# Sums of squares, the scaling of v and the um copies moved from VectorE to ScalarE in the gated-delta heads of a decoder trunk

## The chip, the cores and the metric

The kernel runs on one core of one Trainium2 chip, as one program in one launch. The metric is the device time of one execution in microseconds (us), as a median over several runs; lower is better. The engines are named as the profile names them: PE is TensorE (PEld its weight loads), DVE is VectorE, ACT is ScalarE, POOL is GpSimd, SP is the engine that issues most DMAs.

## What is computed

The reference is a two-layer decoder trunk on 512 tokens of width 1024. Layer 0 is a gated DeltaNet with 8 heads of width 128, layer 1 is differential attention on a shared K/V; each is followed by a squared-ReLU MLP of width 4096, and norms are modulated by a conditioning vector. The change touches layer 0 alone, and there the following:

```python
def l2norm(x):
    xf = x.astype(jnp.float32)
    return (xf * lax.rsqrt(jnp.sum(xf * xf, axis=-1, keepdims=True) + EPS)).astype(x.dtype)
...
    kb = kc * bc[..., None]
    a_mat = jnp.where(strict, jnp.einsum('bhnik,bhnjk->bhnij', kb, kc) * decay, 0.0)
    rhs = jnp.concatenate([vc * bc[..., None], kb * jnp.exp(gcum)[..., None]], axis=-1)
    sol = lax.linalg.triangular_solve(eye + a_mat, rhs, left_side=True, lower=True, unit_diagonal=True)
...
    o = gated_delta_rule(l2norm(q), l2norm(k), v, g, beta).astype(h.dtype)
    o = rmsnorm(o, out_g) * jax.nn.silu(z)
```

Each head therefore needs three sums of squares per token: of q and of k for the l2 norm, and of its output o for the RMS norm. It also needs the inverse of a unit lower-triangular matrix per chunk of tokens.

## The kernel before

Activations lie transposed, 128 features by 512 tokens a tile, in fp32. A projection is split in a high and a low part (fp32r): for each pair of 128-row weight blocks ACT rounds the raw weights to `wh` (L293), DVE or POOL forms the rest `wl` (L284), and PE does three matmuls of 128x512 (L300, L301, L302 in `three`). Raw weights come by SP's DMAs (L291) into three rotating buffers; a buffer is free again when its `wl` has been formed. Beside this runs a queue of dot products that make the modulation vectors (L193 on DVE, its weights by L189 on SP).

The work is not issued in the order of the source. The program is traced first; then a list scheduler with its own cost table puts the instructions of each engine into an order, and every engine runs its own order strictly. A changed instruction can thus shift the order of all engines.

For each of the 8 heads `proj_head(h)` does 72 projection matmuls for q, k and v into three PSUM banks `pj` (tag j has three), and `conv_silu` takes each bank through a four-tap causal convolution: one scaled copy on ACT (L481), three multiply-adds on DVE (L483), a Silu on ACT (L485). A bank is free for the next head only after its three L483. Then `gdn(h)` works in chunks of 128 tokens (the four 128-column units that `uu(t, n)` picks):

- A decay matrix `ex` from `gm` (POOL L528, ACT L531), a matmul (L532), Exp on ACT (L534) and a mask on POOL (L535).
- `natural` transposes k, v and q on PE into bank `pa` (L513; tag a has two banks). `sumsq` (L516) squares a 128x512 tile on ACT (L518) and sums each row per chunk on DVE (L520). It is called for k (`sqk`), q (`sqq`) and later o (`sqo`). Small column operations make `rk` (POOL L543), `sj` (L545, L546) and `nk` (L642); v is scaled by `nk` into `vn` (L648).
- Products of k with k and q (PE L554, L555), masked and scaled into `bq` (DVE L558). The 16x16 diagonal blocks `dc` (L570, L574) go to DRAM and back in another layout (SP L576, L578), are inverted by 15 steps of L584 and L586 on DVE, go through DRAM again (L589, L591), and are spread into the tile `t` (DVE L593).
- `t` is transposed on PE into `z` (L598, L600), and the inverse is doubled from blocks of 16 to 128: with PE products into `pu` (L605, L622), a copy of `pu` to `um` (L607, and L624 for blocks of 32 and 64), products with `z` (L610, L613, L628, L633) and subtractions on DVE (L614, L615, L635, L638). The copy L624 is two pieces of 32x128 and one of 64x256 a head.
- A recurrence over four chunks with the state `st`: five PE products a chunk (L670, L678, L679, L683, L684) with DVE (L676, L681, L688, L690, L660) and ACT (L674, L686) between them. Then the RMS norm of o (`sqo`, L696 to L702) and the output scale (L705 or L707).

While a head's chain runs, PE fills in with projection matmuls of later heads or of the gate (`gate`, L713). `close_block` then multiplies with `a_w_out`, for which `ogh` is made from all heads' outputs (L745).

Of the kernel before, what the change touches and what calls it, by code (L numbers as in the profile page):

```python
# [12 lines left out]
AF = mybir.ActivationFunctionType  # L13
ALU = mybir.AluOpType
AX = mybir.AxisListType
PSUM = bass.MemoryType.PSUM

P = 128
# [3 lines left out]
NT = S // P  # L22
# [63 lines left out]
def trunk_kernel(ctx: ExitStack, tc: tile.TileContext, a, outT):  # L86
    nc = tc.nc
    V, G, A, T = nc.vector, nc.gpsimd, nc.scalar, nc.tensor
# [3 lines left out]
    def nm(s):  # L92
        count[0] += 1
        return f"{s}_{count[0]}"
# [33 lines left out]
    def big(pool, tag, bufs, dt=F32):  # L128
        return pool.tile([P, S], dt, tag=tag, name=nm(tag), bufs=bufs)

    def col(n, name="c"):
        return tp.tile([P, n], F32, tag=f"{name}{n}", name=nm(name))

    def bank(tag):
        return pools["p"].tile([P, S], F32, tag=tag, name=nm("p" + tag), bufs=pools["n"][tag])

    def bc(ap, n):
        return ap.unsqueeze(2).to_broadcast([ap.shape[0], ap.shape[1], n])

    def v3(ap, n=P):  # L140
        return ap.rearrange("p (u f) -> p u f", f=n)
# [231 lines left out]
    for k in range(KT):  # L373
        n = NE[k]
        sq = acc[n]
        if k >= 3:
            sq = m_pool.tile([P, S], F32, tag=f"sq{n}", name=nm("sq"), bufs=2)
# [123 lines left out]
    def uu(t, n):  # L501
        return t[:, n * P:(n + 1) * P]

    def m4(ap):
        return ap.unsqueeze(1).to_broadcast([P, 4, P])
# [3 lines left out]
    def gdn(h):  # L509
        def natural(src, tag="a"):  # L510
            ps = bank(tag)
            for c in range(NT):
                T.transpose(uu(ps, c), uu(src, c), ident)  # L513
            return ps

        def sumsq(src, tag):  # L516
            sq = big(g_pool, {"sqq": "sqk"}.get(tag, tag), 1)
            A.activation(sq, src, AF.Square)  # L518
            ss = col(4, tag)
            V.tensor_reduce(out=ss, in_=v3(sq), axis=AX.X, op=ALU.add)  # L520
            return ss


# [14 lines left out]
        kn = big(g_pool, "kn", 3)  # L538
        A.activation(kn, pk, AF.Copy)
        ssk = sumsq(kn, "sqk")  # L540
        V.tensor_scalar(out=ssk, in0=ssk, scalar1=EPS, scalar2=None, op0=ALU.add)
        rk = col(4, "rk")
# [7 lines left out]
        for n in range(2):  # L550
# [5 lines left out]
            for c in (2 * n, 2 * n + 1):  # L556
                o = (c % 2) * 256
                V.scalar_tensor_tensor(out=v3(bq[n][:, o:o + 256]), in0=v3(ps[:, o:o + 256]), scalar=sj[:, c:c + 1],  # L558
                                       in1=uu(ex, c).unsqueeze(1).to_broadcast([P, 2, P]), op0=ALU.mult, op1=ALU.mult)

        def B(n):
            return bq[n // 2][:, (n % 2) * 256:(n % 2) * 256 + P]
# [6 lines left out]
        for n in range(2):  # L569
            V.tensor_tensor(out=v3(db[:, n * 256:(n + 1) * 256]),  # L570
                            in0=bq[n].rearrange("p (u t f) -> p u t f", u=2, t=2)[:, :, 0, :],
                            in1=m_sub.unsqueeze(1).to_broadcast([P, 2, P]), op=ALU.mult)
# [9 lines left out]
        for s in range(SUB - 1):  # L582
            shp = [32, SUB - 1 - s, s + 1]
            V.tensor_tensor(out=pr[:, s + 1:, :s + 1], in0=mt[:, s, s + 1:].unsqueeze(2).to_broadcast(shp),  # L584
                            in1=xv[:, s, :s + 1].unsqueeze(1).to_broadcast(shp), op=ALU.mult)
            V.tensor_tensor(out=xv[:, s + 1:, :s + 1], in0=xv[:, s + 1:, :s + 1], in1=pr[:, s + 1:, :s + 1],  # L586
                            op=ALU.subtract)
# [6 lines left out]
                        in0=tc_.unsqueeze(2).to_broadcast([P, 4, P // SUB, SUB]),  # L594
                        in1=m4(m_sub).rearrange("p u (b c) -> p u b c", c=SUB), op=ALU.mult)
# [7 lines left out]
        pu = bank("i")  # L603
        for n in range(4):
            T.matmul(uu(pu, n), lhsT=B(n), rhs=uu(t_, n), start=True, stop=True)  # L605
        um = big(g_pool, "um", 1)
# [9 lines left out]
        for b in (32, 64):  # L616
            parts = [(slice(lo, lo + b), slice(lo + b, lo + 2 * b)) for lo in ((0, 64) if b == 32 else (0,))]
            pu = bank("i")
            um = big(g_pool, "um", 1)
            for p0, p1 in parts:  # L620
                for n in range(4):
                    T.matmul(pu[p1, n * b:(n + 1) * b], lhsT=B(n)[p0, p1], rhs=uu(t_, n)[p0, p0], start=True, stop=True)  # L622
            for p0, p1 in parts:
                V.tensor_copy(um[p1, 0:4 * b], pu[p1, 0:4 * b])  # L624
            pz = bank("i")
            for p0, p1 in parts:
                for n in range(4):
                    T.matmul(pz[p0, n * b:(n + 1) * b], lhsT=um[p1, n * b:(n + 1) * b], rhs=uu(z, n)[p1, p1],  # L628
                             start=True, stop=True)
            if b == 32:  # L630
                p0, p1 = parts[0]
                for n in range(4):
                    T.matmul(pz[p1, n * b:(n + 1) * b], lhsT=uu(z, n)[p1, p1], rhs=um[p1, n * b:(n + 1) * b],  # L633
                             start=True, stop=True)
                V.tensor_tensor(out=v3(t_)[p1, :, p0], in0=v3(t_)[p1, :, p0],  # L635
                                in1=v3(pz[p1, 0:4 * b], b), op=ALU.subtract)
            for p0, p1 in parts:
                V.tensor_tensor(out=v3(z)[p0, :, p1], in0=v3(z)[p0, :, p1], in1=v3(pz[p0, 0:4 * b], b),  # L638
                                op=ALU.subtract)

        nk = col(4, "nk")
# [3 lines left out]
        G.tensor_tensor(out=v3(kn), in0=v3(kn), in1=bc(kd, P), op=ALU.mult)  # L645
        pv = natural(vT[h])
        vn = big(g_pool, "vn", 4)
        V.tensor_tensor(out=v3(vn), in0=v3(pv), in1=bc(nk, P), op=ALU.mult)  # L648

        ssq = sumsq(natural(qT[h]), "sqq")  # L650
        V.tensor_scalar(out=ssq, in0=ssq, scalar1=float(P), scalar2=EPS * P, op0=ALU.mult, op1=ALU.add)
        rq = col(4, "rq")
# [40 lines left out]
        yield  # L693

        so = sumsq(o, "sqo")
        V.tensor_tensor(out=so, in0=so, in1=rq, op=ALU.mult)  # L696
        V.tensor_tensor(out=so, in0=so, in1=rq, op=ALU.mult)
# [31 lines left out]
    for h in range(H):  # L729
        proj_head(h)  # L730
        heads.append(gdn(h))
        next(heads[h])
        next(heads[h])
        if h:
            next(heads[h - 1], None)
# [136 lines left out]
    scale = 128 ** -0.5  # L872
# [138 lines left out]
```

## Time and profile before

| what | value |
|---|---|
| median of 3 runs | 1384.9 us (1381.57 to 1387.92) |
| profiled execution, its own time | 1381.92 us |
| its span, first to last instruction | 1380.1 us |
| mean granted TensorE clock | 0.986 |
| busy: PE, PEld, DVE, ACT, POOL | 95%, 80%, 62%, 38%, 34% of the span |

The profile is of one execution. Its page gives busy time by engine, the same in 40 slices of 34.5 us, and the costliest groups of instructions. Further views of the trace answer by group of instructions (line, engine, operation, tiles, count, total busy time in us, mean of one in ns, then idle time before them and what ended it), by wait (who waited for whom: total us, times, longest), by stretch of time, and as a timeline. Times within the span are counted from its start. A busy PE is not a PE at its peak: matmuls are pipelined and their ends are modelled.

The stage of the change lies between about 84 us, when the first head's chain starts, and about 392 us, when the last head's output is scaled.

### The profile page before, as it was taken

The numbers are of one execution on the slowest core, as the hardware profiler recorded it, in microseconds if no ns is written. First come the engines' busy times: TensorE is split into PE (matmuls) and PEld (weight loads), VectorE is DVE, ScalarE is ACT, GpSimd is POOL, SyncE is SP. The second block draws the span as 40 slices with busy tenths as digits, with TensorE's granted clock in tenths as the row PEclk, the third lists the DMA queues.
The fourth block names the chain that finished last, engine by engine and source line by source line (L and its number), as shares of the span: only waits on it lengthen the run. The fifth ranks groups of instructions, "written<-read, shape, count | busy, mean of one in ns | idle before, by whom it ended". The sixth has DMA issues, their size and how long they took to land. (4 is left out here: it accounts for less than half of the span.)

```text
span 1380.1 us, 19204 instructions
## 1 busy us (share of the span) xinstructions
PE 1309.7 (95%) x7240; PEld 1101.4 (80%) x7240; DVE 850.9 (62%) x1688; ACT 529.1 (38%) x951; POOL 471.4 (34%) x281
## 2 busy tenths in 40 slices
PE   4887998999999999999999999999999999999997
PEld 3665787777789888888888987888798888888886
DVE  6989899899846987778861687777552110031113
ACT  3394344443424533225332354444344322143221
POOL 3324132222004544444444012232135444444441
PEclk9997999999999999999999999999999999999998
DMA  9632223225542776776753233222113233233221
GB/s 314 212 90 57 81 78 81 74 72 147 175 151 65 266 239 225 242 236 219 241 165 100 81 100 104 65 66 66 61 62 123 92 96 103 92 100 99 92 76 62
DMA packets 113212, 174.97 MB, mean 127 GB/s; under 512 B 16384, under 2 KB 56992, under 8 KB 113120
## 3 DMA queue, kind: packets, MB, share of 16 engines
q1 hardware_dynamic: 112416, 172.92, 39.5%
q8 instruction: 57, 0.93, 0.3%
q10 hardware_dynamic: 704, 0.83, 0.2%
q14 instruction: 35, 0.29, 0.1%
HBM read 170.04 MB, written 2.62 MB: 125 GB/s over the span
## 5 line engine op out<-in xcount | busy, mean ns | idle before, releaser
L284 POOL TENSOR_TENSOR wl<-raw,wh 128x1024 fp32r<-128x1024 f32 (+1 forms) x137 | 329.3, 2404 | 392.9 <-ACT wh L293 392.9
L293 ACT ACTIVATE wh<-raw 128x1024 fp32r<-128x1024 f32 (+2 forms) x217 | 216.0, 996 | 502.0 <-PE pj L301 250.1
L300 PE MATMUL pj<-h,wh 128*128 128x512 f32 (+1 forms) x816 | 290.9, 360 | 16.0 <-ACT h L278 5.5
L301 PE MATMUL pj<-h,wh 128*128 128x512 f32 (+1 forms) x816 | 292.6, 359 | 0.0
L302 PE MATMUL pj<-h,wl 128*128 128x512 f32 (+1 forms) x816 | 290.4, 358 | 1.1 <-DVE wl L284 1.1
L193 DVE SCALAR_TENSOR_TENSOR mw<-mw,one,cs 128x1024 f32<-128x1024 f32 x96 | 210.1, 2202 | 47.5 <-ACT one L213 47.2
L300 PEld LDWEIGHTS pj<-h,wh 128*128 128x128 f32 x816 | 155.9, 192 | 37.2 <-ACT h L278 7.5
L302 PEld LDWEIGHTS pj<-h,wl 128*128 128x128 f32 x816 | 156.6, 192 | 19.4 <-DVE wl L284 2.4
L301 PEld LDWEIGHTS pj<-h,wh 128*128 128x128 f32 x816 | 156.9, 192 | 17.9 <-DVE h L279 0.3
L301 PE MATMUL pj<-u,wh 128*128 128x512 f32 (+1 forms) x448 | 160.9, 359 | 0.0
L302 PE MATMUL pj<-u,wl 128*128 128x512 f32 (+1 forms) x448 | 160.9, 359 | 0.0
L300 PE MATMUL pj<-u,wh 128*128 128x512 f32 (+1 forms) x448 | 160.8, 359 | 0.0
L346 DVE SCALAR_TENSOR_TENSOR x<-pj,mod,x 128x256 f32<-128x256 f32 (+1 forms) x53 | 30.2, 584 | 152.2 <-PE pj L302 152.2
L284 DVE TENSOR_TENSOR wl<-raw,wh 128x1024 fp32r<-128x1024 f32 (+2 forms) x80 | 84.5, 1058 | 18.7 <-ACT wh L293 18.6
L300 PEld LDWEIGHTS pj<-u,wh 128*128 128x128 f32 x448 | 84.6, 189 | 12.7 <-issue 0.2
L301 PEld LDWEIGHTS pj<-u,wh 128*128 128x128 f32 x448 | 84.6, 189 | 12.5
L302 PEld LDWEIGHTS pj<-u,wl 128*128 128x128 f32 x448 | 84.6, 189 | 12.5
L767 DVE SCALAR_TENSOR_TENSOR pj<-pj,r 128x512 f32<-128x512 f32 x32 | 21.6, 690 | 52.2 <-ACT r L766 52.0
L301 PE MATMUL pn<-h,wh 128*128 128x512 f32 x128 | 49.8, 389 | 0.0
L300 PE MATMUL pn<-h,wh 128*128 128x512 f32 x128 | 49.8, 389 | 0.0
L300 PE MATMUL pm<-h,wh 128*128 128x512 f32 x128 | 49.8, 389 | 0.0
L302 PE MATMUL pm<-h,wl 128*128 128x512 f32 x128 | 49.8, 389 | 0.0
(298 smaller groups left out, 2371.7 us busy)
## 6 DMA issues: line engine op xcount, KB each, us to landing
raw<-in_mlp_w_dram SPq DMA_DIRECT2D x128, 512.0 KB, 3.7
mw<-in_mod_wT_dram SPq DMA_DIRECT2D x96, 512.0 KB, 4.7
raw<-in_a_w_in_dram SPq DMA_DIRECT2D x96, 128.0 KB, 2.6
mw<-in_kv_mod_wT_dram SPq DMA_DIRECT2D x16, 512.0 KB, 5.1
raw<-in_kv_w_dram SPq DMA_DIRECT2D x16, 512.0 KB, 3.3
x<-in_xT_dram SPq DMA_DIRECT2D x16, 256.0 KB, 6.0
raw<-in_a_w_in_dram SPq DMA_DIRECT2D x16, 256.0 KB, 2.9
raw<-in_a_w_out_dram SPq DMA_DIRECT2D x8, 512.0 KB, 4.3
```

What stands on the lines that cost most here:

```text
L193: V.scalar_tensor_tensor(out=w, in0=w, scalar=one, in1=cs, op0=ALU.mult, op1=ALU.mult, accum_out=raw_mod[:, c:c + 1])
L284: (V if n else G).tensor_tensor(out=out, in0=x, in1=hi.bitcast(F32), op=ALU.subtract)
L293: A.activation(wh, raw, AF.Copy)
L300: T.matmul(ps, lhsT=wh, rhs=xh, start=first, stop=False, skip_group_check=skip)
L301: T.matmul(ps, lhsT=wh, rhs=xl, start=False, stop=False, skip_group_check=skip)
L302: T.matmul(ps, lhsT=wl, rhs=xh, start=False, stop=last, skip_group_check=skip)
L346: V.scalar_tensor_tensor(out=x[d][:, sl], in0=ps[j][:, sl], scalar=mod[:, gt + d:gt + d + 1], in1=x[d][:, sl], op0=ALU.mult, op1=ALU.add)
L767: V.scalar_tensor_tensor(out=ps[j], in0=ps[j], scalar=0.0, in1=r, op0=ALU.max, op1=ALU.mult)
```

## The change

Four things move from DVE to ACT, all in `gdn`; nothing else is edited.

- `sumsq` no longer squares a whole tile on ACT and sums on DVE. ACT squares each of the four 128x128 chunks with an accumulated output, which is the sum. One ACT and one DVE instruction become four ACT instructions with an accumulator each.
- The copies of `pu` to `um` (L624) become ACT copies of the same shapes.
- The scaling of v into `vn`, one DVE multiply of 128x512, becomes four ACT copies of 128x128, each with a per-partition scale (L649 in the changed file; after it all line numbers are one higher).

```diff
         def sumsq(src, tag):
             sq = big(g_pool, {"sqq": "sqk"}.get(tag, tag), 1)
-            A.activation(sq, src, AF.Square)
             ss = col(4, tag)
-            V.tensor_reduce(out=ss, in_=v3(sq), axis=AX.X, op=ALU.add)
+            for c in range(NT):
+                A.activation(uu(sq, c), uu(src, c), AF.Square, accum_out=ss[:, c:c + 1])
             return ss
...
             for p0, p1 in parts:
-                V.tensor_copy(um[p1, 0:4 * b], pu[p1, 0:4 * b])
+                A.activation(um[p1, 0:4 * b], pu[p1, 0:4 * b], AF.Copy)
...
         vn = big(g_pool, "vn", 4)
-        V.tensor_tensor(out=v3(vn), in0=v3(pv), in1=bc(nk, P), op=ALU.mult)
+        for c in range(NT):
+            A.activation(uu(vn, c), uu(pv, c), AF.Copy, scale=nk[:, c:c + 1])
```

The heads still come in the same order, but the scheduler puts out another order within each engine. Three places follow. In them a name is that of a tile with its running number, so numbers differ between the two programs for the same tile.

First PE, at the first transpose of `t` (L598, head 0), before: `pj` are projection banks, `h` the activations, `cv` the convolved tiles, `wh` and `wl` the weight parts.

```order
L300 MATMUL pj_1475<-h_172,wh_1506 128x512
L513 MATMUL pa_1392<-mask,cv_1220 128x128 x4
L301 MATMUL pj_1475<-h_173,wh_1506 128x512
L513 MATMUL pa_1399<-mask,cv_1214 128x128 x4
L532 MATMUL pa_1608<-gm_1609,m_gtr 128x512
L532 MATMUL pa_1608<-gm_1612,m_gtr 128x512
L598 MATMUL pi_687<-mask,t_685 128x128 x4
L605 MATMUL pi_694<-t_685,bq_623 128x128 x2
```

The same place on PE in the changed program:

```order
L301 MATMUL pj_1498<-h_181,wh_1588 128x512
L302 MATMUL pj_1498<-h_180,wl_1590 128x512
L300 MATMUL pj_1498<-h_182,wh_1588 128x512
L301 MATMUL pj_1498<-h_183,wh_1588 128x512
L302 MATMUL pj_1498<-h_182,wl_1590 128x512
L598 MATMUL pi_689<-mask,t_687 128x128 x4
L605 MATMUL pi_696<-t_687,bq_625 128x128 x2
```

Before, PE comes to L598 in the middle of head 3's second block of weights; now it has done two of head 3's three banks with all four blocks. Counted over the whole order, 264 projection matmuls (L300 to L302) stand ahead of it before, and 306 now. No earlier or later head changes its turn.

Second DVE, at the first low part `wl` of head 3's weights, before (`pr`, `xv` and `mt` belong to the inversion of the 16x16 blocks):

```order
L541 TENSOR_SCALAR sqk_1248<-sqk_1248 128x4
L586 TENSOR_TENSOR xv_648<-xv_648,pr_649 32x8x8
L586 TENSOR_TENSOR xv_895<-xv_895,pr_896 32x15
L284 TENSOR_TENSOR wl_1482<-raw_1476,wh_1480 128x768
L584 TENSOR_TENSOR pr_649<-mt_646,xv_648 32x7x9
```

The same tile on DVE in the changed program:

```order
L483 SCALAR_TENSOR_TENSOR cv_1236<-pj_1105,cols,cv_1236 128x511
L546 TENSOR_TENSOR sj_876<-sj_876,beta 128x4
L284 TENSOR_TENSOR wl_1507<-raw_1501,wh_1505 128x768
L584 TENSOR_TENSOR pr_651<-mt_648,xv_650 32x15
L558 SCALAR_TENSOR_TENSOR bq_879<-pa_881,sj_876,ex_857 128x256
```

The cast has moved ahead of the whole inversion of head 0 and of head 1's `bq`. Counted from L475, the last instruction that all heads share, the first L593 is the 111th DVE instruction before and the 109th now; one `wl` stands between the two before, four now.

Third the copies `um` of head 0. Before they stood on DVE, behind the subtraction that follows the block-16 step:

```order
L615 TENSOR_TENSOR z_692<-z_692,pi_706 128x512
L624 COPY um_714<-pi_713 32x128 x2
L584 TENSOR_TENSOR pr_896<-mt_893,xv_895 32x2x14
L584 TENSOR_TENSOR pr_1282<-mt_1279,xv_1281 32x14x2
L193 SCALAR_TENSOR_TENSOR mw_1188,raw_mod<-mw_1188,one_1567,cs 128x1024
```

In the changed program they stand on ACT:

```order
L534 ACT_TABLE_LOAD
L534 ACTIVATE ex_1643<-pa_1633 128x512
L624 ACTIVATE um_716<-pi_715 32x128 x2
L293 ACTIVATE wh_1979<-raw_1975 128x768
L485 ACT_TABLE_LOAD
L485 ACTIVATE cv_1621<-cv_1621 128x512
L624 ACTIVATE um_744<-pi_743 64x256
```

The first two pieces stand behind an Exp with its table load, the third behind a weight cast and a Silu with its table load. Both programs hold 24 table loads in all.

## Prediction

> **What bounds the kernel now.** I read the page first, for its slices of the span.
>
> ```profile
> span 1380.1 us, 19204 instructions
> PE   4887998999999999999999999999999999999997
> DVE  6989899899846987778861687777552110031113
> ACT  3394344443424533225332354444344322143221
> PEclk9997999999999999999999999999999999999998
> ```
>
> PE is at nine tenths nearly everywhere, but its first slices are not, and these are the slices in which DVE is full (slice 3 to 11, some 70 to 390 us) and in which the granted clock drops once, to 7. Next I asked for stretches of time: the columns are length, then PE, PEld, DVE, ACT and POOL busy in us with their instructions, then granted clock, DMA share and GB/s.
>
> ```profile
> 90.00:130.00 40.00, 29.67 (x126) 22.66 (x124) 34.97 (x112) 24.33 (x45) 17.16 (x16) 0.79 0.16 39
> 130.00:400.00 270.00, 254.94 (x1734) 206.71 (x1735) 231.36 (x652) 111.91 (x203) 59.90 (x45) 0.98 0.39 111
> 400.00:1380.00 980.00, 960.97 (x5122) 822.07 (x5120) 511.02 (x811) 350.70 (x643) 367.23 (x200) 1.00 0.39 126
> ```
>
> The heads' stage is the first two rows. There DVE is busy 87% and 86% of the time, ACT 61% and 41%, and PE lacks 10.3 us (40 - 29.67) and 15.1 us (270 - 254.94). After 400 us DVE is at 52%, and PE lacks 2% of the time; nothing of the change lies there. So what can be won is what PE lacks before 400 us. The first part in steps of 10 us shows a second loss:
>
> ```profile
> 90.00:100.00 10.00, 8.23 (x42) 6.46 (x41) 6.25 (x17) 8.40 (x17) 3.33 (x3) 0.96 0.30 86
> 100.00:110.00 10.00, 7.45 (x33) 5.57 (x31) 9.53 (x28) 5.42 (x10) 4.33 (x4) 0.69 0.05 7
> 110.00:120.00 10.00, 7.17 (x28) 5.60 (x28) 9.19 (x27) 6.55 (x11) 6.35 (x5) 0.65 0.06 10
> 120.00:130.00 10.00, 6.82 (x27) 5.03 (x25) 10.00 (x46) 3.96 (x7) 3.14 (x4) 0.84 0.24 51
> ```
>
> PE's busy time times the clock it lacked (8.23 x 0.04 + 7.45 x 0.31 + 7.17 x 0.35 + 6.82 x 0.16) is 6.2 us. With the idle 10.3 us, PE loses 16.5 us here, while DVE is at 9.5, 9.2 and 10 of 10 and hardly any DMA moves. The waits name the cause (who waited for whom; total us, times, longest):
>
> ```profile
> PE pi L598 <- DVE t L593: 5.5, 4, 2.6
> PE pj L300 <- DVE cv L483: 4.5, 3, 2.6
> PE pr L513 <- POOL o L702: 2.4, 1, 2.4
> PEld pj L300 <- ACT cv L485: 3.1, 1, 3.1
> SPq L291 <- DVE wl L284: 121.6, 31, 21.0
> ACT wh L293 <- PE pj L301: 38.7, 17, 5.2
> ```
>
> PE waits mostly for DVE. The fifth row is the longer reach of it: SP could not load the next raw weights, once for 21 us, since DVE had not come to the `wl` that frees their buffer. The timeline of DVE has these casts at
>
> ```profile
> 84.82 3.46 DVE L284 TENSOR_TENSOR wl<-raw,wh 128x768 fp32r<-128x768 f32 x2
> 117.85 0.94 DVE L284 TENSOR_TENSOR wl<-raw,wh 128x768 fp32r<-128x768 f32 x1
> ```
>
> and nothing between, which is the time of the idle DMA and the low clock. DVE's queue is thus the bound of the heads' start, and in what follows DVE and PE share it.
>
> **What leaves DVE.** From 84 to 392 us:
>
> ```profile
> L520 DVE TENSOR_REDUCE sqo<-sqo 128x4 f32<-128x512 f32 x8 | 5.4, 678 | 1.2 <-ACT sqo L518 1.1
> L648 DVE TENSOR_TENSOR vn<-pa,nk 128x512 f32<-128x512 f32 x8 | 5.4, 674 | 0.0
> L520 DVE TENSOR_REDUCE sqk<-sqk 128x4 f32<-128x512 f32 x8 | 5.4, 670 | 4.2 <-ACT sqk L518 4.2
> L520 DVE TENSOR_REDUCE sqq<-sqk 128x4 f32<-128x512 f32 x8 | 5.3, 667 | 0.0
> L624 DVE COPY um<-pi 32x128 f32<-32x128 f32 x16 | 4.6, 290 | 3.0 <-PE pi L622 2.6
> L624 DVE COPY um<-pi 64x256 f32<-64x256 f32 x8 | 3.4, 428 | 6.7 <-PE pi L622 6.7
> ```
>
> The sum is 29.5 us of busy time, or 3.7 us a head, a tenth of what DVE does there (34.97 + 231.36 = 266.3 us). With the `um` go 9.7 us (3.0 + 6.7) in which DVE stood still for PE with other heads' work behind it.
>
> **What comes to ACT.** No ACT square of 128x128 with an accumulator stands in the trace. The nearest rows:
>
> ```profile
> L518 ACT ACTIVATE sqk<-kn 128x512 f32<-128x512 f32 x8 | 5.0, 624 | 0.1
> L914 ACT ACTIVATE on<-po 128x256 f32<-128x256 f32 x16 | 6.1, 380 | 4.7 <-PE po L302 4.6
> L914 ACT ACTIVATION_READ_ACCUMULATOR on<-po 128x1 f32 x16 | 3.2, 199 | 0.0
> L904 ACT ACTIVATE aTh<-pt 128x256 fp32r<-128x256 f32 x4 | 1.5, 381 | 0.2 <-PE pt L902 0.2
> L674 ACT ACTIVATE o<-pr 128x128 f32<-128x128 f32 x8 | 2.2, 275 | 15.1 <-PE pr L670 15.1
> L686 ACT ACTIVATE o<-pr,eg_all 128x128 f32<-128x128 f32 x24 | 8.8, 367 | 34.6 <-PE pr L684 34.4
> ```
>
> and the timeline of an accumulated square of 128x256 with what follows it:
>
> ```profile
> 861.90 0.37 ACT L914 ACTIVATE on<-po 128x256 f32<-128x256 f32 x1
> 862.17 0.20 ACT L914 ACTIVATION_READ_ACCUMULATOR on<-po 128x1 f32 x1
> 862.26 0.58 ACT L892 ACTIVATE pr<-pss,mx 128x384 f32<-128x384 f32 x1
> ```
>
> The next instruction starts 0.36 us after the square, so most of the read is overlapped. For 128 columns less, the rows of L904 and L674 differ by 0.106 us, so a piece holds ACT for some 0.25 us and four for 1.0; without any overlap they take 4 x (0.275 + 0.199) = 1.9 us. Against the one square of 0.62 us that goes, 24 calls add 9 us, or up to 31; I take 10, since overlap is what the timeline shows. `vn` is 32 copies at L686's 0.367 us, 11.7 us. The `um` are 16 copies at no more than 0.275 us and 8 at no more than 0.381 us, 7.4 us. ACT gains about 29 us, or 50 at the upper end, on 136.2 us (24.33 + 111.91) in 310: it goes from 44% to 53% or 60%. As throughput that is covered by its idle time. Its latency in the chains is not: for k and q, a square and a sum (0.62 + 0.67 us and a signal between) become about 1.0 to 1.9 us on one engine, level with before; for o, only the last chunk's piece (0.25 to 0.47 us) follows the recurrence, where 0.62 + 0.68 us did.
>
> A rule speaks against the move: the Trainium skill, "ScalarE: Activation LUTs", section "Rules for kernel authors", says to use VectorE and not ScalarE for plain adds and multiplies. For these shapes the rows do not bear it out: 0.275 us on ACT (L674, 128x128) beside 0.290 us on DVE (L624, 32x128). By that rule the moves would cost more than they free; what that makes of the time is the third rival.
>
> **What moves, and the sum.** Everything behind `sqk` on DVE moves up, and the scheduler used it: four of head 3's `wl` casts now stand ahead of the first L593 where one did, at the same number of DVE instructions; PE's order has 306 projection matmuls ahead of the first L598 instead of 264. Successive ones start 0.23 us apart:
>
> ```profile
> 94.00 0.40 PE L300 MATMUL pj<-h,wh 128*128 128x512 f32 x1
> 94.23 0.39 PE L301 MATMUL pj<-h,wh 128*128 128x512 f32 x1
> ```
>
> - Start of the heads: 42 x 0.23 = 9.7 us of PE work that now lies where PE lost 16.5 us. Ends: nothing, if PE waits there as long as before; 16.5, if all is filled. I take 9.7, which the order itself gives. SP's raw loads for it come sooner, as their buffers are freed by those casts.
> - 130 to 400 us: of PE's 15.1 us of waits I take a third, 5 us, since L593, L483 and the recurrence's DVE steps wait a tenth less in DVE's queue; ends 0 and 15.1.
> - End of the stage: PE stood 2.4 us for POOL's L702 at the last head, and that chain shortens by 0.8 us (1.30 less 0.47).
> - Against: waits on ACT grow. ACT gets 7 us more in the 40 us of the start (three heads' k, q and v: 3 x (2 x 0.4 + 1.47)), where PEld waited 3.1 us for a Silu; I charge those 3 us a second time. Ends: 0, and the third rival.
>
> Together -9.7 - 5 - 0.8 + 3 = -12.5 us. The profiled execution took 1381.9 us, which makes 1369.4; it lay 3.0 us under the median of 1384.9, so against the median I forecast 1372. This case alone gives 1362 to 1378.
>
> The clock is not a term of its own: 9.7 us is at full clock and lies within 16.5. In the rows the clock fell to 0.69 and 0.65 where PE was busy 7.4 and 7.2 of 10 us. The Trainium skill, "TensorE: Matmul & The Clock Gate", section "Part 1: The HAM clock gate (the "warmup" mystery)", says that the clock is throttled by default and released by sustained activity. By that rule the 6.2 us return as soon as PE stays busy there, and the sum would reach -18.7.
>
> **The rivals.**
>
> *The cover runs out* (no change). The 42 matmuls are no new work: before, they filled PE between the steps of later chains, where PE is at its fullest. If PE then waits for L628, L679 or L683 as long as it saved at the start, 9.7 us come back and the sum is -2.8 us: 1382. For it: PE lacks only 15.1 us in 270 with DVE at 86%, so it is near its own bound. Against it: DVE is a tenth shorter, so those chains are faster too.
>
> *All is filled* (much faster). PE loses 16.5 + 15.1 = 31.6 us in the stage; without any of it, 1353. Against: chains of PE, DVE and ACT steps remain.
>
> *ACT's strict order* (slower). The 24 `um` copies lie on the path PE - copy - PE (L622 to L628), and on ACT they now stand behind weight casts that themselves wait for PE (38.7 us in 17 waits, up to 5.2 us) or behind a table load. The price of one such predecessor is
>
> ```profile
> L293 ACT ACTIVATE wh<-raw 128x768 fp32r<-128x768 f32 x32 | 26.8, 839 | 35.6 <-DMA raw<-in_a_w_in_dram 21.9 <-PE pj L301 12.9 <-PE pa L301 0.6
> L534 ACT ACT_TABLE_LOAD x7 | 9.0, 1283 | 1.9 <-PE pa L532 1.8
> ```
>
> Where one table load or cast (mean 1.06 us) stands before each copy, 24 x 1.06 = 25 us; less the 12.5, 1397. It decides from 0.5 us a copy on (12.5 / 24). For it: the order of head 0 shows just this. Against: DVE made those copies wait as well, and ACT is idle half the time.
>
> That the change doesn't do what it says is out: the order shows the DVE instructions gone and 24 table loads in both.
>
> **How the numbers follow.** A measurement of this kernel can tell about 0.5%, 6.9 us, from no change. I give the forecast 0.50 and *all is filled* 0.12, both faster: 0.62. *The cover runs out* gets 0.22, *ACT's strict order* 0.16; its reason stands in the order, but DVE's full queue stands in the trace. The range leaves out the far part of the second and the fourth case: from 1357, a few us above all filled, to 1391, half way between no gain and 1397.
>
> **What would show it.** Right: between 90 and 130 us DVE's casts come at some 100 us and not at 118, the clock stays above 0.9 and PE is busy 36 or more of 40 us; the last L702 comes some 12 us sooner, and after it all is shifted by that. Wrong: the start is filled but PE in 130 to 400 us lacks more than 15 us, with waits of L628 or L598; or PEld L628 waits for ACT `um` by over 10 us in all; or ACT's pieces hold it for 0.45 us each, and the `pj` banks wait for L485.

## The result, and the profile after

The changed kernel takes 1368.72 us (median of 4 runs, 1367.7 to 1369.39), the kernel before 1384.29 us beside it (1381.57 to 1387.92). The ratio is 0.9885, with a 95% interval of 0.9861 to 0.991: faster by 15.6 us, where 12.5 were forecast. The profiled execution took 1367.7 us. One run of a kernel further down, the one with the `um` copies alone on ScalarE, took 3518 us and is not in its ratio. (In the changed kernel all lines behind the scaling of v are numbered one higher: before's L702 is L703.)

The page of the changed kernel:

```profile
span 1365.9 us, 19395 instructions
PE 1304.3 (95%) x7240; PEld 1097.0 (80%) x7240; DVE 829.7 (61%) x1632; ACT 558.8 (41%) x1175; POOL 471.1 (34%) x281
PE   4888999999999999999999999999999999999997
PEclk9999999899999999999999999999999999999998
```

ACT has 29.7 us more than before (558.8 - 529.1), as forecast, and DVE 21.2 less. The dip of the clock at the start of the heads (slice 4) is gone; a small one stands in slice 8. The heads' stage in stretches, first the two of the prediction, then the start in steps:

```profile
90.00:130.00 40.00, 33.34 (x166) 25.51 (x165) 33.43 (x114) 31.28 (x100) 20.61 (x14) 0.96 0.30 78
130.00:400.00 270.00, 259.94 (x1802) 213.01 (x1803) 219.16 (x606) 137.75 (x378) 55.33 (x47) 0.98 0.38 109
```

```profile
90.00:100.00 10.00, 9.04 (x52) 6.99 (x51) 5.80 (x16) 9.64 (x33) 5.07 (x4) 1.00 0.17 38
100.00:110.00 10.00, 6.85 (x28) 4.88 (x28) 9.53 (x29) 7.24 (x23) 3.46 (x4) 0.83 0.31 85
110.00:120.00 10.00, 9.48 (x52) 7.57 (x51) 8.48 (x21) 9.15 (x30) 8.56 (x5) 1.00 0.49 137
120.00:130.00 10.00, 7.97 (x39) 6.06 (x38) 9.62 (x50) 5.25 (x18) 3.52 (x3) 1.00 0.22 53
```

At the start PE gains 3.7 us of busy time (33.34 against 29.67) and the clock goes from 0.79 to 0.96; from 130 to 400 us it gains 5.0 us (259.94 against 254.94). Four of DVE's casts for head 3 now stand ahead of the first L593, as the order had it; the first comes 13 us sooner than the one of before:

```profile
104.97 0.95 DVE L284 TENSOR_TENSOR wl<-raw,wh 128x768 fp32r<-128x768 f32 x1
...
116.88 0.96 DVE L284 TENSOR_TENSOR wl<-raw,wh 128x768 fp32r<-128x768 f32 x1
```

Of the waits in the stage, these are the ones that the prediction spoke of (us in total, times, longest):

```profile
PE pj L300 <- DVE cv L483: 2.3, 3, 1.6
PE pr L513 <- POOL o L703: 1.7, 1, 1.7
PE pi L598 <- DVE t L593: 1.2, 1, 1.2
PEld pi L628 <- ACT um L624: 2.9, 8, 0.4
```

PE's waits for L593 fall from 5.5 us to 1.2, those for L483 from 4.5 to 2.3. L628 waits 2.9 us in all for the copy, now on ACT; for the copy on DVE it had waited 1.3 before:

```profile
PEld pi L628 <- DVE um L624: 1.3, 4, 0.4
```

What the work costs on ACT:

```profile
L649 ACT ACTIVATE vn<-pa,nk 128x128 f32<-128x128 f32 x32 | 9.6, 372 | 9.1 <-PE pa L513 9.1
L520 ACT ACTIVATE sqk<-kn 128x128 f32<-128x128 f32 x32 | 9.5, 307 | 0.1
L624 ACT ACTIVATE um<-pi 32x128 f32<-32x128 f32 x16 | 4.3, 270 | 11.6 <-PE pi L622 11.3
L624 ACT ACTIVATE um<-pi 64x256 f32<-64x256 f32 x8 | 3.0, 381 | 10.1 <-PE pi L622 10.1
```

The end of the stage can be dated by POOL's last output scale and by the first matmul of the norm in `close_block`. Before:

```profile
389.85 1.90 POOL L702 TENSOR_TENSOR o<-o,ro 128x512 f32<-128x512 f32 x1 [0.37 <-DVE ro L701]
...
416.69 0.50 PE L260 MATMUL pn<-ones,acc 128*128 128x1 f32 x4
```

and after:

```profile
371.27 1.35 POOL L703 TENSOR_TENSOR o<-o,ro 128x512 f32<-128x512 f32 x1 [0.34 <-DVE ro L702]
...
402.27 0.50 PE L260 MATMUL pn<-ones,acc 128*128 128x1 f32 x4
```

The scale comes 18.6 us sooner; the matmuls behind it, which PE had to do in both, leave 14.4 of these. The shift of 14.4 us is, to 0.2 us, the difference of the two profiled executions (1381.9 - 1367.7 = 14.2). All of the gain lies ahead of this point, in the stage where the prediction looked for it. The question is which part of the change makes it, and how.

### The profile page after: what moved, and what is told of

Read it like the earlier page. It is cut to its first block, busy times and chain, and to the rows that moved or that the text cites. A ratio compares the mean times of both kernels' runs of the same rounds, so it can differ in the third digit from the quotient of the medians.

```text
span 1365.9 us, 19395 instructions
## 1 busy us (share of the span) xinstructions
PE 1304.3 (95%) x7240; PEld 1097.0 (80%) x7240; DVE 829.7 (61%) x1632; ACT 558.8 (41%) x1175; POOL 471.1 (34%) x281
## 5 line engine op out<-in xcount | busy, mean ns | idle before, releaser
L300 PE MATMUL pj<-h,wh 128*128 128x512 f32 (+1 forms) x816 | 291.2, 360 | 12.4 <-ACT h L278 6.7
L302 PE MATMUL pj<-h,wl 128*128 128x512 f32 (+1 forms) x816 | 290.5, 358 | 1.9 <-DVE wl L284 1.9
L300 PEld LDWEIGHTS pj<-h,wh 128*128 128x128 f32 x816 | 155.7, 191 | 33.3 <-ACT h L278 8.8
L302 PEld LDWEIGHTS pj<-h,wl 128*128 128x128 f32 x816 | 156.2, 192 | 20.1 <-DVE wl L284 2.6
L302 PE MATMUL pj<-u,wl 128*128 128x512 f32 (+1 forms) x448 | 160.9, 359 | 0.0
L300 PE MATMUL pj<-u,wh 128*128 128x512 f32 (+1 forms) x448 | 160.8, 359 | 0.0
L300 PEld LDWEIGHTS pj<-u,wh 128*128 128x128 f32 x448 | 84.6, 189 | 12.7 <-issue 0.2
L302 PEld LDWEIGHTS pj<-u,wl 128*128 128x128 f32 x448 | 84.6, 189 | 12.5
L300 PE MATMUL pn<-h,wh 128*128 128x512 f32 x128 | 49.8, 389 | 0.0
L302 PE MATMUL pn<-h,wl 128*128 128x512 f32 x128 | 49.8, 389 | 0.0
L300 PE MATMUL pm<-h,wh 128*128 128x512 f32 x128 | 49.8, 389 | 0.0
```

The costliest lines, as they stand in the source:

```text
L300: T.matmul(ps, lhsT=wh, rhs=xh, start=first, stop=False, skip_group_check=skip)
L302: T.matmul(ps, lhsT=wl, rhs=xh, start=False, stop=last, skip_group_check=skip)
```

## The experiments

Two theories stood against each other at first. *The load:* VectorE's queue is full in this stage, and every microsecond off it helps. *The place:* only some of the moved steps matter, for what hangs on them. All ratios are against the kernel before, run on the same chip beside the experiment (medians of 1383.6 to 1385.2 us).

**One part at a time.** The diff is that of the change, reduced to one of its three parts, and once all but `um`:

```
sums only, against the kernel before:
-            A.activation(sq, src, AF.Square)
-            V.tensor_reduce(out=ss, in_=v3(sq), axis=AX.X, op=ALU.add)
+            for c in range(NT):
+                A.activation(uu(sq, c), uu(src, c), AF.Square, accum_out=ss[:, c:c + 1])
v only, against the kernel before:
-        V.tensor_tensor(out=v3(vn), in0=v3(pv), in1=bc(nk, P), op=ALU.mult)
+        for c in range(NT):
+            A.activation(uu(vn, c), uu(pv, c), AF.Copy, scale=nk[:, c:c + 1])
um only, against the kernel before:
-                V.tensor_copy(um[p1, 0:4 * b], pu[p1, 0:4 * b])
+                A.activation(um[p1, 0:4 * b], pu[p1, 0:4 * b], AF.Copy)
um back, against the changed kernel:
-                A.activation(um[p1, 0:4 * b], pu[p1, 0:4 * b], AF.Copy)
+                V.tensor_copy(um[p1, 0:4 * b], pu[p1, 0:4 * b])
```

Sums only: 

> Only the sums of squares go to ScalarE; the um copies and the scaling of v stay on VectorE. My theory: what counts is the work that leaves VectorE's queue, above all at the start of the heads, where the low parts of the weights wait behind it. The sums are 16.1 us of the 29.5 us, and 3 of the 4 us or so that leave the queue before the first L593, so this gives the larger half of the 15.6 us: 8 to 11 us less than before, with the casts of head 3 at some 105 us. Rival, the um copies: their leaving ends VectorE's own waits for PE (9.7 us), and they lie on the path; then this gives under 5 us. Rival, the order alone: each part gives a new order and a gain that has nothing to do with its size.

v only: 

> Only the scaling of v goes to ScalarE. My theory: 5.4 us of VectorE work leave, of them 2 us early; 2 to 4 us less than before. Rival, the order alone: anything from 10 us less to 5 us more.

um only: 

> Only the um copies go to ScalarE. My theory: 8.0 us of VectorE work leave, and 9.7 us in which VectorE waited for PE, but all of it after the first L593, where PE has little to gain; 2 to 5 us less than before. Rival, the um copies carry the gain: 8 us less or more. Rival, ScalarE's strict order: slower than before, with PE's weight loads of L628 waiting over 10 us for um.

um back: 

> The changed kernel with the um copies back on VectorE (sums and v stay on ScalarE). My theory: 11 to 14 us less than before, that is 2 to 4 us more than the changed kernel. Rival, the um copies carry the gain: 7 us less than before or smaller. Rival, they cost on ScalarE: faster than the changed kernel.

Measured:

| kernel | median us | ratio | 95% interval |
|---|---|---|---|
| sums only | 1365.24 | 0.9869 | 0.9854 to 0.9885 |
| v only | 1381.36 | 0.9979 | 0.9969 to 0.9989 |
| um only | 1379.24 | 0.9968 | 0.9957 to 0.9978 |
| um back (sums and v) | 1368.47 | 0.9888 | 0.9875 to 0.9901 |
| the change (all three) | 1368.72 | 0.9885 | 0.9861 to 0.991 |

The sums alone bring all of the gain; their interval overlaps with that of the whole change. v and `um` bring 0.2 and 0.3% alone and nothing on top of the sums, though they take 13.4 of the 29.5 us off DVE. That speaks against the load as such.

**The same work on every engine, another result used.** These two kernels do the same work for the sums: ScalarE squares in four accumulated pieces and VectorE sums the squares as well. In the first, which has v and `um` on ScalarE, the kernel goes on with ScalarE's sums; in the second, which has them on VectorE, with VectorE's. The other set of sums goes into a column that nothing reads; no part of the result is left out.

```
first, against the changed kernel:
+            spare = col(4, "spare")
+            V.tensor_reduce(out=spare, in_=v3(sq), axis=AX.X, op=ALU.add)
second, against the kernel before:
-            A.activation(sq, src, AF.Square)
+            spare = col(4, "spare")
+            for c in range(NT):
+                A.activation(uu(sq, c), uu(src, c), AF.Square, accum_out=spare[:, c:c + 1])
```

First: 

> The changed kernel, with VectorE summing every square once more into a spare column that nothing reads (24 reductions of 0.67 us, 16 us of VectorE time as before the change; the outputs do not depend on them). Theory A, VectorE's queue is the price: what the sums gained was their 16 us on VectorE, so with them back at least two thirds of the gain goes: 1379 to 1385 us. Rival B, the chains' form: the gain comes from the accumulated pieces being one step on one engine instead of two steps with a signal between, and a reduction on no chain costs little: 1367 to 1373 us.

Second: 

> The kernel before, with ScalarE squaring in four accumulated pieces into a spare column that nothing reads, and VectorE summing the squares as before: ScalarE's added work of the sums without VectorE's relief (the outputs do not depend on the spare). Theory A: ScalarE's time is covered, so no change, within 4 us of the kernel before: 1380 to 1388 us. Rival C, ScalarE's pieces have a price of their own, the 3 us or more that the forecast charged: slower, 1387 to 1394 us. Rival B, the pieces' form is the gain: faster by over 5 us, under 1379 us.

The first took 1366.84 us, ratio 0.9872 (0.9854 to 0.989): the gain stays whole with VectorE's sums back. They do stand in its trace, 16.2 us of them:

```profile
L522 DVE TENSOR_REDUCE spare<-sqk 128x4 f32<-128x512 f32 x16 | 10.8, 674 | 5.7 <-ACT sqk L520 5.6
L522 DVE TENSOR_REDUCE spare<-sqo 128x4 f32<-128x512 f32 x8 | 5.4, 675 | 0.5 <-ACT sqo L520 0.5
```

The load theory falls with this run: in this order the sums' time on VectorE cost nothing. The second took 1397.43 us, ratio 1.0094 (1.0077 to 1.0111), slower than before by 13 us, more than any theory gave it. The two differ by 30.6 us; v and `um`, worth a few us by the table, cannot make that up. A large part of it is seen on ACT. In the second kernel, `kn` of the third head is there at 116.8 us, and its square runs at 151.5 (start, duration; in brackets the idle time before and who ended it):

```profile
116.17 0.59 ACT L541 ACTIVATE kn<-pa 128x512 f32<-128x512 f32 x1
...
150.86 0.28 ACT L676 ACTIVATE o<-pr 128x128 f32<-128x128 f32 x1 [9.94 <-PE pr L672]
151.17 0.31 ACT L521 ACTIVATE sqo<-o 128x128 f32<-128x128 f32 x1
...
151.48 0.29 ACT L521 ACTIVATE sqk<-kn 128x128 f32<-128x128 f32 x1
```

ACT stood idle for 9.94 us just ahead of `o` (L676), waiting for PE. The reason is ACT's own order. The rows of the second kernel, then of the first (the number ahead is the row's place in that order; `o_787` and `o_790` are the first head's output, `kn_1264` and `kn_1270` belong to the third head):

```
89 L541 ACTIVATE kn_1264<-pa_1259 128x512
106 L676 ACTIVATE o_787<-pr_788 128x128
108 L521 ACTIVATE sqk_1266,spare_1268<-kn_1264 128x128 x4

95 L520 ACTIVATE sqk_1272,sqk_1273<-kn_1270 128x128 x4
115 L677 ACTIVATE o_790<-pr_791 128x128
```

In the second, the scheduler put the third head's square behind the first head's recurrence; every engine runs its order strictly, so a square that could run (DVE had last read its buffer by 114.5 us) waited for another head. From there the heads run in pairs: the third head's chain starts 35 us late, and for the fifth and seventh head 33.7 and 22.9 us pass from the end of `kn` to the end of the epsilon step on k's sum. Between 140 and 200 us PE is busy 49.91 of 60 us:

```profile
140.00:200.00 60.00, 49.91 (x363) 40.24 (x362) 50.87 (x155) 29.06 (x87) 18.82 (x16) 0.91 0.11 27
```

So for the sums it is not how much an engine does that moves the time. What is left is what the head's chain hangs on, and the order that the scheduler makes of it; the pair does not part these two, since each kernel has its own order.

**Which sums.** The change's sums for o alone, for k and q, and for k alone (`if tag == ...` around the two forms of `sumsq`).

o: 

> The kernel before, with the sums of o alone moved to ScalarE (8 reductions, 5.4 us off VectorE); those of k and q stay. If a microsecond off VectorE is worth the same anywhere (18 us for 16 us), a third of the gain of the sums: 6 us, 1378 us. If the head of the chains counts (k's sum stands ahead of all that follows), nothing: 1382 to 1385 us. If the tail of the chains counts (o's sum is the last link to the end of the stage), more than half: 1366 to 1374 us.

k and q: 

> The kernel before, with the sums of k and q alone moved to ScalarE (16 reductions, 10.7 us off VectorE); that of o stays. If a microsecond off VectorE is worth the same anywhere: 12 us, 1372 us. If the head of the chains counts, nearly all of the gain: 1365 to 1368 us. If the tail counts, less than half: 1376 to 1383 us.

k: 

> The kernel before, with the sums of k alone moved to ScalarE (8 reductions, 5.4 us off VectorE); those of q and o stay. Theory L, latency of k's sum: what was gained is that k's sum, on which the head's chain hangs, no longer stands in VectorE's queue; q's sum is on no chain before the output. Then nearly all of the 14.4 us of k and q together: 1368 to 1374 us. Theory S, the shared buffer: the squares of k and q share one buffer, so a head's square of k waits for VectorE's sum of the q before, and this remains here; less than half: 1378 to 1385 us.

| sums on ScalarE | median us | ratio | 95% interval |
|---|---|---|---|
| o | 1386.25 | 1.0012 | 1.0001 to 1.0024 |
| k and q | 1370.41 | 0.9896 | 0.9879 to 0.9913 |
| k | 1375.97 | 0.9927 | 0.9915 to 0.994 |

o, the last link to the end of the stage, brings nothing alone. k, on which the head's chain hangs, brings some two thirds of what k and q do (8.7 of 14.4 us by the medians, 0.73 of 1.04% by the ratios); the rest comes with q, which is needed only at the head's end and was not moved by itself. Neither theory of the third expectation is met cleanly: 1375.97 lies between them.

**The buffer that k's and q's squares share.** q's square goes into o's buffer:

```
-            sq = big(g_pool, {"sqq": "sqk"}.get(tag, tag), 1)
+            sq = big(g_pool, {"sqq": "sqo"}.get(tag, tag), 1)
```

> The kernel before, with the square of q written into the buffer of o's square and no longer into that of k's. No engine does more or less; all sums stay on VectorE. Theory S, the shared buffer: a third or more of the gain, 1370 to 1379 us. Theory L: no gain from it; the scheduler's order changes a little with the buffers, within 4 us of the kernel before: 1380 to 1388 us.

1388.02 us, ratio 1.0021 (1.001 to 1.0032). Freeing the buffer gains nothing. With no engine's work changed, this kernel with its new order is 0.2% slower.

**The filled start by itself.** The kernel before, with head 3's low parts formed by POOL:

```
             for k0 in range(0, KT, 2):
+                lo_on[0] = 0 if h == 3 else 1
                 head_pair(ps, head_weights(h, k0), k0)
+                lo_on[0] = 1
```

> The kernel before, with the low parts of head 3's four weight pairs formed by POOL and not by VectorE (4 casts, 3.8 us off VectorE); all sums stay on VectorE. It tests the forecast's largest term by itself: the order has 262 projection matmuls ahead of the first head's transposes, as many as the changed kernel and 46 more than the kernel before. If the start of the heads is worth what the forecast put there (9.7 us, 8.7 us read from the changed kernel's trace), 1374 to 1378 us. If what is filled at the start is given back later, as the rival The cover runs out has it, 1381 to 1387 us.

(Its counts leave out 48 matmuls that the forecast's 264 and 306 hold; counted alike, 262 is 310, 4 more than in the changed kernel.) 1385.49 us, ratio 1.0 (0.9988 to 1.0011): nothing, although the start is filled. Its stretches beside those of the kernel before show where it goes. The kernel before:

```profile
90.00:140.00 50.00, 39.46 (x210) 31.12 (x209) 43.27 (x132) 27.55 (x51) 21.79 (x17) 0.80 0.26 65
140.00:200.00 60.00, 59.08 (x441) 48.99 (x441) 52.28 (x156) 27.08 (x48) 13.46 (x11) 1.00 0.26 70
200.00:320.00 120.00, 109.81 (x738) 88.86 (x737) 109.29 (x332) 51.82 (x92) 31.89 (x26) 0.99 0.29 78
320.00:420.00 100.00, 95.81 (x626) 79.16 (x625) 71.60 (x166) 35.65 (x66) 10.61 (x7) 0.98 0.51 157
```

The one with the casts on POOL:

```profile
90.00:140.00 50.00, 41.92 (x236) 33.79 (x236) 42.41 (x133) 30.68 (x53) 27.11 (x21) 0.90 0.29 75
140.00:200.00 60.00, 56.93 (x422) 47.63 (x420) 51.39 (x154) 23.36 (x46) 12.63 (x12) 0.91 0.21 55
200.00:320.00 120.00, 110.49 (x729) 88.51 (x727) 107.08 (x323) 51.55 (x93) 30.68 (x26) 0.97 0.29 78
320.00:420.00 100.00, 96.06 (x611) 79.42 (x611) 72.48 (x169) 34.59 (x65) 10.55 (x7) 0.97 0.52 161
```

Sums only:

```profile
90.00:140.00 50.00, 42.12 (x234) 32.82 (x233) 43.58 (x133) 30.17 (x90) 22.59 (x15) 0.86 0.36 93
140.00:200.00 60.00, 57.62 (x446) 47.36 (x441) 53.69 (x160) 31.74 (x87) 15.69 (x14) 1.00 0.26 69
200.00:320.00 120.00, 116.37 (x834) 94.53 (x833) 109.43 (x337) 61.63 (x178) 31.79 (x27) 1.00 0.34 91
320.00:420.00 100.00, 96.64 (x641) 83.37 (x639) 67.79 (x157) 41.34 (x88) 15.42 (x10) 1.00 0.49 151
```

The change:

```profile
90.00:140.00 50.00, 42.73 (x255) 33.13 (x253) 43.35 (x133) 37.07 (x108) 25.65 (x17) 0.97 0.30 82
140.00:200.00 60.00, 57.25 (x429) 46.92 (x430) 54.15 (x162) 34.92 (x110) 15.46 (x13) 1.00 0.33 86
200.00:320.00 120.00, 116.29 (x819) 94.02 (x819) 101.02 (x309) 65.36 (x190) 30.09 (x27) 0.96 0.29 76
320.00:420.00 100.00, 96.12 (x622) 83.14 (x622) 66.33 (x149) 41.19 (x87) 15.75 (x10) 1.00 0.50 162
```

PE's loss in a stretch is its idle time and its busy time times the clock that it lacked, as in the prediction (39.46 us busy of 50 at 0.80 is 10.5 + 7.9 = 18.4):

| lost us | 90-140 | 140-200 | 200-320 | 320-420 | all |
|---|---|---|---|---|---|
| before | 18.4 | 0.9 | 11.3 | 6.1 | 36.7 |
| before, casts on POOL | 12.3 | 8.2 | 12.8 | 6.8 | 40.1 |
| sums only | 13.8 | 2.4 | 3.6 | 3.4 | 23.2 |
| the change | 8.6 | 2.8 | 8.4 | 3.9 | 23.7 |

The casts on POOL save 6.1 us at the start and lose 7.3 in the next stretch: this fits the rival *The cover runs out*, by which PE then lacks the matmuls that it had already done. The sums save much less at the start than the change does, but 7.7 us from 200 to 320 us, with DVE as full as before (109.43 and 109.29 of 120 us): PE does 834 instructions there instead of 738. Of the change's 8.4 us in that stretch, 4.7 are the clock's (116.29 x 0.04), in this one execution.

**k's sum without VectorE in its chain.** A last theory was that k's sum waits its turn in VectorE's strict order. One step of it was left there, the epsilon of L541:

```
-        V.tensor_scalar(out=ssk, in0=ssk, scalar1=EPS, scalar2=None, op0=ALU.add)
+        G.tensor_scalar(out=ssk, in0=ssk, scalar1=EPS, scalar2=None, op0=ALU.add)
```

> The sums of k, q and o on ScalarE alone (v and um stay on VectorE, 1365.2 us), and in addition the small step that adds the epsilon to k's sum (L541, 4 values a row) moved from VectorE to POOL, so that between k's square and the power on POOL nothing of the chain stands in VectorE's strict queue. Theory L, k's sum waits for its turn in VectorE's queue: the wait that is left there goes, and the time falls by 2 to 7 us more: 1358 to 1363 us. Theory O, the time follows the order that the scheduler finds and no single queue position: no gain on top, 1363 to 1372 us.

1371.59 us, ratio 0.99 (0.9883 to 0.9916): no gain over the sums alone (0.9869), rather a loss. Theory L is not borne out in this form.

The traces say the same more directly. From the end of `kn` to the end of the epsilon step, the last five heads together take 40.9 us before, 16.7 in the change, 31.2 with sums only and 14.6 in this kernel. But with `um` only they take 24.8, with little gain, and in the first kernel of the pair 39.3, with all of it. There the fourth head's `kn` and epsilon step (L543 there) lie 16 us apart:

```profile
156.03 0.60 ACT L541 ACTIVATE kn<-pa 128x512 f32<-128x512 f32 x1 [1.75 <-PE pr L686]
...
172.35 0.15 DVE L543 TENSOR_SCALAR sqk<-sqk 128x4 f32<-128x4 f32 x1
```

So the time does not follow how long k's sum takes to come.

**From head to head.** Where the gain lies is dated by L593 (L595 in three of the kernels), which writes `t` once a head. Its row gives the count, the shortest, median and longest in ns, and the starts of the first and the last. Before, the change, sums only, the first and the second kernel of the pair, and the casts on POOL:

```profile
L593 DVE TENSOR_TENSOR t<-tc,mask x8: 670/674/694, 129.5 to 354.8; 128x512 f32<-128x512 f32 x8
L593 DVE TENSOR_TENSOR t<-tc,mask x8: 671/686/1175, 129.2 to 336.3; 128x512 f32<-128x512 f32 x8
L593 DVE TENSOR_TENSOR t<-tc,mask x8: 669/680/693, 131.3 to 338.2; 128x512 f32<-128x512 f32 x8
L595 DVE TENSOR_TENSOR t<-tc,mask x8: 669/674/960, 131.3 to 338.6; 128x512 f32<-128x512 f32 x8
L595 DVE TENSOR_TENSOR t<-tc,mask x8: 672/680/694, 135.7 to 371.9; 128x512 f32<-128x512 f32 x8
L595 DVE TENSOR_TENSOR t<-tc,mask x8: 673/687/1737, 132.1 to 358.0; 128x512 f32<-128x512 f32 x8
```

The first head gets there no sooner in the change (129.2 us against 129.5), and in the others later. The last gets there 16 to 19 us sooner in the three kernels that gain: seven steps of 29.6 us from head to head, where before had 32.2, the casts on POOL 32.3 and the second kernel 33.7. So the chain of the first head is no faster; the heads follow each other faster. Projection work that PE did ahead at the start may be a part of that, but the casts on POOL show that it is not enough.

What is settled: the sums of k and q make the gain. It is not one lucky order: the six kernels that take both from ScalarE have ratios from 0.9869 to 0.99, the six that take both from VectorE from 0.9968 to 1.0094, and k alone lies between (0.9927). The time that the sums took on VectorE does not explain it, nor does the filled start alone. ScalarE's pieces and the shared buffer brought nothing by themselves, each tried in one order only. What stays open is how the change shortens the step from head to head, and which rows of the new order do it. The experiments could change dependencies, from which the scheduler made its own order each time; an order was never held fixed while a chain was changed, or the other way round.

## Why the prediction was right, and where its reasons were not

The time, the sign and the stretches were right. That the total came so near is in part luck: the largest term is worth nothing by itself, and the sums of k and q, which make the gain, had no term of their own. Point by point:

- *What bounds the kernel.* That what could be won was what PE loses in this stage fits: from 90 to 420 us the losses fell by 13.0 us (36.7 less 23.7) in the profiled execution, which is 14.2 us shorter.
- *Start of the heads, -9.7 us.* In the changed kernel's trace the start saves 8.7 us from 90 to 130 us: 3.7 of idle time, and 5.0 of the clock (6.2 less 1.2, which is 6.85 x 0.17; the other three steps are at 1.00). The size is near, the step failed all the same. It took 42 matmuls moved ahead for a gain of their own, and the casts on POOL move as many and gain nothing. The first head's `t` comes no sooner either. With the sums alone, PE saves more from 200 to 320 us (7.7 us) than at the start (4.6). That the filled start counts once the later waits go is possible, but not shown.
- *The clock is not a term of its own.* As a sum this held: the start saved 8.7 us, and not 9.7 with 6.2 on top. What the text did not say is that more than half came through the clock: 5.0 us, and only 3.7 as filled time. The Trainium skill, "TensorE: Matmul & The Clock Gate", section "Part 1: The HAM clock gate (the "warmup" mystery)", ties the clock to the PE's recent activity; these rows agree in direction (0.65 at 7.17 us busy of 10 before, 1.00 at 9.48 now), and of the 6.2 us that its rule would return, 5.0 did. The busy share of 10 us alone does not give the clock, as the last section shows.
- *130 to 400 us, -5 us.* Exactly 5.0 us of busy time, a third of 15.1; as the third was only taken, that is luck. The reason given, that steps "wait a tenth less in DVE's queue", is the one that fell: with the sums' 16.2 us back on VectorE the gain stays. In its place the trace shows PE waiting less for L593 (1.2 us) and L483 (2.3 us) and heads that follow each other in 29.6 us; what in the new order does it is open.
- *k and q "level with before".* Their chain on ACT is about as long as on two engines, as forecast: four pieces at 0.29 us against 0.62 + 0.67. So the prediction gave them no term of their own, only a share in the shorter queue, and the sums of k and q alone made 14.4 us. A step of equal length can still be ordered elsewhere by the scheduler; this was the largest miss.
- *End of the stage, -0.8 us.* PE's wait for the last scaling went from 2.4 to 1.7 us, near what was forecast, but o's sums alone gain nothing that the runs could show.
- *ACT's waits, +3 us.* Not seen where it was put: PEld's wait for a Silu (3.1 us before) did not double; in the change such waits come to 0.9 us in all. L628 waits 2.9 us for the `um` copies, but 1.3 of these it waited before, so 1.6 are new. Why moving `um` adds nothing on top (0.9888 without, 0.9885 with) is open.
- *The rule against the move*, of the Trainium skill, "ScalarE: Activation LUTs", section "Rules for kernel authors", names adds and multiplies among others. The prediction set it beside copies, and these are no dearer on ACT: 0.270 and 0.381 us against 0.290 and 0.428 on DVE. The one plain multiply among the moved steps, the scaling of v, agrees with it: 9.6 us on ACT in all, 5.4 on DVE. On top of the sums neither of these two moves gained anything.
- *ACT's strict order* did not come with the `um` copies (0.4 us at the longest), but its mechanism is real: the second kernel of the pair, 13 us slower than before, shows it with k's square.

Of the marks named ahead, the clock (0.96 in the mean, with 0.83 in one step) and the last scaling came (371.3 instead of 389.9 us, 18.6 us sooner where some 12 were named), PE's 36 of 40 us did not (33.34), and the casts came at 105 to 117 us and not all near 100.

## What to carry to other kernels

Where a scheduler orders the work and every engine runs its order strictly, the time that a step takes on a full engine does not tell what moving it is worth: put the step back as a spare whose result nothing reads, and see whether the gain stays. A gain that an order promises at one place, such as matmuls moved into a gap, is counted only after looking at where those matmuls had been cover before. And of a change in several parts, time the parts: here one of three made the whole gain. A row that stands once in every round, as L593 does once a head, shows whether the first round comes sooner or the rounds follow each other faster.

## What the runs showed of the hardware

Accumulated squares of 128x128 follow each other on ACT every 0.29 us from SBUF, their 0.19 us reads of the accumulator between them almost hidden. In the changed kernel:

```profile
91.67 0.30 ACT L520 ACTIVATE sqk<-kn 128x128 f32<-128x128 f32 x1
91.87 0.19 ACT L520 ACTIVATION_READ_ACCUMULATOR sqk<-kn 128x1 f32 x1
91.96 0.30 ACT L520 ACTIVATE sqk<-kn 128x128 f32<-128x128 f32 x1
```

And the same busy share of PE over 10 us does not give the same clock here. With sums only:

```profile
110.00:120.00 10.00, 7.99 (x30) 6.52 (x30) 10.00 (x24) 7.43 (x25) 6.98 (x4) 0.50 0.28 67
```

Here PE is busy 7.99 us at a clock of 0.50; in the changed kernel's last step above, 7.97 us at 1.00.
